# Rotation tables on VectorE, a third convolution buffer and a second buffer of carried states in a two-layer encoder kernel

## The chip, the core and the metric

One core of a Trainium2 chip runs the whole program. The metric is the device time of one execution in microseconds. A core has five engines that run their own instruction streams: TensorE (PE, with its weight loads as PEld), VectorE (DVE), ScalarE (ACT), GpSimd (POOL) and SyncE (SP), whose work here is to issue DMA transfers. An engine runs its instructions in the order in which they were written into its stream; between engines semaphores keep the order.

## The reference

The kernel computes two layers of an encoder over 2048 positions of 1024 features in float32. Only the first layer is touched by the change:

```
h = x + even_layer(rms_norm(x, g0))
even_layer(h):                       # h: [2048, 1024]
    u_a, z_a, v_b, g_b, z_b = split(h @ w_in, 5 x 512)
    y_a = s5(u_a)                    # 32 groups x 16 channels, 64 complex states a group
    y_b = silu(layer_norm(conv31(v_b * sigmoid(g_b)) + conv_b))
    return concat(y_a * silu(z_a), y_b * silu(z_b)) @ w_out
s5(u): s_t = A s_{t-1} + Bbar u_t    # diagonal complex A, per group
       y   = Re(C s) + D u ;  g = gelu(y) ;  return g * sigmoid(g @ w_glu + b_glu)
...
out = rms_norm(h + odd_layer(rms_norm(h, g1)), final_g)   # second layer: sparse attention
```

## The kernel before

The first layer works on the sequence in two halves of 1024 positions (h = 0, 1). `norm(h)` normalises, transposes and splits the rows into a high and a low part (hh, hl), so that a float32 product is made of three matmuls (lines 121 to 123). A projection (`proj`) makes 128 output channels of one half: 8 feature blocks x 2 position blocks x 3 = 48 matmuls of 128x512, into two PSUM tiles ps_p of a pool with four buffers; so a third projection in a row needs that the first one's results have been read. Its weights come in two loads of 256 KB into the staging tile wst (two slots), are cast to wh by ScalarE (line 113) and get their low part wl by a subtraction on GpSimd (line 114), which frees the slot.

The program of half 0 is: `vg(0)` and `vg(1)`, the convolution branch of channel blocks 0 and 1; the tables of the scan, `s5_tables`; four projections `uproj` to uT; the scan `s5_main`; `vg(2)`, `vg(3)`; eight projections `zproj` to zt. In `vg` the gate's projection goes through a sigmoid on ScalarE into sg, the value's projection is multiplied by sg into hc on VectorE, and the convolution is one tensor_scalar and thirty multiply-adds cvo of 128x1024 on VectorE (lines 69 and 72). Where the text says channel 2 it means the channel block of `vg(2)`.

`s5_tables` makes rot, the rotation tables [128, 16, 2, 128] (cosine and sine of the powers), by doubling: in step i the first w columns are rotated by a fixed angle into the next w. It needs four products, one subtraction and one addition per pass, all on GpSimd (`gp_`) before the change; eight passes with w of 1, 2, 4, 8, 16, 32, 32, 32. The scratch tiles ra and rb have one buffer each, under the tags gt and ga; the later tiles q1, q2, and gt and ga of the table quarters, use the same tags. Then come eight quarters: products gt and ga on VectorE, ps_g and ps_h on TensorE, rec on ScalarE, and hs. All is written to HBM (rec_d) and read back by `s5_main` as rg, rt and ry.

`s5_main` takes the input U, which was written to HBM as u_d and read back in eight transfers. For each of eight pairs of groups TensorE makes ps_v, VectorE rotates it by rt (s5t), scans it and rotates it back into sprev (the states at the start of each step, with the carried one in front), and TensorE makes ps_y from sprev and U.

The order of each engine is not the program's: a scheduler orders all engines at build time with a simulated time line, by priority in program order (with a few raised priorities for weight loads, norms, the glu part and the scan of half 1), whenever the tiles that an instruction needs have a free buffer. A changed buffer count or engine so changes the order of all of the first layer. In the second half the same parts follow, with `uproj(1)` and `s5_main(1)` in the middle of the convolution's channels, and with `glu` and `out` at the end. The names in the pool ev, by its tag, are sg, zt, uT, ys and part of xr; the pool is opened in line 446, and sprev in line 534.

Of the kernel before, what the change touches and what calls it, by code (L numbers as in the profile page):

```python
# [11 lines left out]
F32 = mybir.dt.float32  # L12
# [6 lines left out]
ALU = mybir.AluOpType  # L19
# [4 lines left out]
P = 128  # L24
# [6 lines left out]
KC = 128  # L31
# [153 lines left out]
def s5_tables(k, sp, big, ec, S5, rec_d, hs_d, rho, ident, pt):  # L185
# [40 lines left out]
    gp_ = nc.gpsimd  # L226
    for i in range(7):
        m = 1 << i
        w = min(m, 32)
        c0 = cs[:, 1 + i, :, None].to_broadcast([P, 16, w])  # L230
        s0 = sn[:, 1 + i, :, None].to_broadcast([P, 16, w])
        for o in range(0, m, w):
            ra = sp.tile([P, 16, 32], F32, tag="gt", name="ra")[:, :, 0:w]
            rb = sp.tile([P, 16, 32], F32, tag="ga", name="rb")[:, :, 0:w]
            ore = rot[:, :, 0, m + o:m + o + w]
            oim = rot[:, :, 1, m + o:m + o + w]
            ire = rot[:, :, 0, o:o + w]
            iim = rot[:, :, 1, o:o + w]
            k.vtt(ore, ire, c0, ALU.mult, gp_)
            k.vtt(ra, iim, s0, ALU.mult, gp_)  # L240
            k.vtt(oim, ire, s0, ALU.mult, gp_)
            k.vtt(rb, iim, c0, ALU.mult, gp_)
            k.vtt(ore, ore, ra, ALU.subtract, gp_)
            k.vtt(oim, oim, rb, ALU.add, gp_)
    nc.sync.dma_start(
        rec_d[:, :, 768:1024].rearrange("g p c -> p g c"),
        rot.rearrange("p g a c -> p g (a c)"))
# [181 lines left out]
def layer0(k, A, h1_d, ident, vec, dbg):  # L429
# [4 lines left out]
    with ExitStack() as ctx:  # L434
        pool = lambda name, bufs, **kw: ctx.enter_context(tc.tile_pool(name=name, bufs=bufs, **kw))
# [7 lines left out]
        xp = pool("xp", 4)  # L443
        sm = pool("sm", 2)
        pers = pool("pers", 1)
        ev = pool("ev", 2)
        big = pool("big", 3)
        hcp = pool("hcp", 2)
        pt = pool("pt", 2, space=PSUM)
# [14 lines left out]
        pl = {}  # L464
# [63 lines left out]
        def s5_main(h, U, pps):  # L528
            sh = [P, 2, 2, KC]
            for pp in pps:  # L530
                pv = p5.tile(sh, F32, tag="p5v", name="ps_v", bufs=1)
                t1 = pl["s5"].tile([P, 2, 2, 2, KC], F32, tag="s5", name="s5t1")
                w = pl["s5"].tile([P, 2, 2, KC], F32, tag="s5w", name="s5w")
                sp_ = pl["s5"].tile([P, 2, 2, KC + 1], F32, tag="sprev", name="sprev", bufs=1)
                rg = pl["rc"].tile([P, 2, 256], F32, tag="rg", name="rg")
                rt = pl["rc"].tile([P, 2, 256], F32, tag="rt", name="rt")
                ry = pl["rc"].tile([P, 2, 512], F32, tag="ry", name="ry")
                rv = rec_d[2 * pp:2 * pp + 2].rearrange("g p c -> p g c")
                nc.sync.dma_start(rg, rv[:, :, 0:256])
                nc.sync.dma_start(rt, rv[:, :, 768:1024])  # L540
                nc.sync.dma_start(ry, rv[:, :, 256:768])
                for q in range(2):
                    gp = 2 * pp + q
                    for ri in range(2):
                        for eo in range(2):
                            nc.tensor.matmul(
                                pv[64 * eo:64 * eo + 64, q, ri],
                                rg[:, q, ri * 128 + 64 * eo:ri * 128 + 64 * eo + 64],
                                U[:, 2 * gp + eo], start=True, stop=True)
                C = rt[:, :, None, 0:128].to_broadcast(sh)  # L550
                S = rt[:, :, None, 128:256].to_broadcast(sh)
                a, b = t1[:, 0], t1[:, 1]
                win = w
                k.vtt(a, pv, C, ALU.mult)
                k.vtt(b, pv, S, ALU.mult)
                k.vtt(win[:, :, 0], a[:, :, 0], b[:, :, 1], ALU.add)
                k.vtt(win[:, :, 1], a[:, :, 1], b[:, :, 0], ALU.subtract)
                for q in range(2):
                    gp = 2 * pp + q
                    for ri in range(2):  # L560
                        nc.vector.tensor_tensor_scan(
                            out=w[:, q, ri], data0=rho[:, gp:gp + 1].to_broadcast([P, KC]),
                            data1=win[:, q, ri], initial=carry[:, gp, ri:ri + 1],
                            op0=ALU.mult, op1=ALU.add)
                nc.gpsimd.tensor_copy(sp_[:, :, :, 0:1], carry[:, 2 * pp:2 * pp + 2, :, None])
                k.vtt(a, w, C, ALU.mult)
                k.vtt(b, w, S, ALU.mult)
                k.vtt(sp_[:, :, 0, 1:], a[:, :, 0], b[:, :, 1], ALU.subtract)
                k.vtt(sp_[:, :, 1, 1:], a[:, :, 1], b[:, :, 0], ALU.add)
                if h == 0:  # L570
                    nc.gpsimd.tensor_copy(carry[:, 2 * pp:2 * pp + 2, :, None], sp_[:, :, :, KC:])
                uv = U[:, 4 * pp:4 * pp + 4].rearrange("p (q e) c -> p q e c", e=2)
                for eo in range(2):
                    py = p5.tile([P, 2, KC], F32, tag="p5y", name="ps_y", bufs=1)
                    rows = slice(64 * eo, 64 * eo + 64)
                    for q in range(2):
                        nc.tensor.matmul(py[:, q], ry[:, q, 256 + 128 * eo:384 + 128 * eo],
                                         uv[:, q, eo], start=True, stop=False)
                        nc.tensor.matmul(py[:, q], ry[rows, q, 0:128],
                                         sp_[rows, q, 0, 0:KC], start=False, stop=False)  # L580
                        nc.tensor.matmul(py[:, q], ry[rows, q, 128:256],
                                         sp_[rows, q, 1, 0:KC], start=False, stop=True)
                    nc.scalar.activation(uv[:, :, eo], py, AF.Gelu_apprx_tanh)
                if pp % 4 == 3:
                    g0 = (pp // 4) * 16
                    for j in range(NJ):
                        nc.sync.dma_start(
                            g_d[h, g0 * 16:g0 * 16 + 256, j].rearrange("(g c) k -> c g k", c=16),
                            U[16 * j:16 * j + 16, g0:g0 + 16])
# [105 lines left out]
        with tc.tile_pool(name="sp", bufs=1) as sp:  # L695
            s5_tables(k, sp, big, ec, A, rec_d, hs_d, rho, ident, pt)
        pl["s5"] = pool("s5", 2)
        pl["rc"] = pool("rc", 2)
        U = uproj(0, hT)
        s5_main(0, U, range(8))  # L700
        vg(0, hT, cvos[0], 2)
        vg(0, hT, cvos[0], 3)
# [14 lines left out]
        with tc.high_priority(offset=300):  # L717
            s5_main(1, U, range(0, 8))
# [666 lines left out]
def body(tc, A, out, dbg=None, stop=None):  # L1385
    nc = tc.nc
    k = K(tc)
    with ExitStack() as ctx:
        cst = ctx.enter_context(tc.tile_pool(name="cst", bufs=1))
        dpool = ctx.enter_context(tc.tile_pool(name="dscr", bufs=1, space=DRAM))  # L1390
        ident = cst.tile([P, P], F32, name="ident")
        make_identity(nc, ident)
        identr = cst.tile([P, P], F32R, name="identr")
        nc.vector.tensor_copy(identr, ident)
        vec = cst.tile([P, VEC_N], F32, name="vec")
        nc.sync.dma_start(vec, A["vec"])
        dbg = dbg or {}
        scr = lambda n, s, t=F32: dbg[n] if n in dbg else dpool.tile(s, t, name=n + "_d")
        h1_d = scr("h1", [L, D])
        layer0(k, A, h1_d, ident, vec, dbg)  # L1400
        if stop == "l0":
            return
        S = {"q": scr("q", [L, D]), "z": scr("z", [L, D]), "qi": scr("qi", [L, 512]), "att": scr("att", [L, D]),
             "kh": scr("kh", [4, P, L]), "kl": scr("kl", [4, P, L]), "v": scr("v", [L, 256]),
             "mask": scr("mask", [16, P, L], BF16), "sc": scr("sc", [16, P, L]), "hT": scr("hT", [NF, 2, P, HALF])}
        layer1(k, A, h1_d, S, ident, identr, vec)
        layer1_out(k, A, h1_d, S, out, ident)
# [53 lines left out]
```

## Time and profile before

| | us |
|---|---|
| median of three runs | 3005.96 (3002.47 to 3012.47) |
| profiled execution | 3008.15 |
| its span in the trace | 3006.3 |
| TensorE busy in the span | 2754.0 (92%) |
| VectorE busy | 2127.9 (71%) |
| ScalarE busy | 1694.8 (56%) |
| GpSimd busy | 1118.3 (37%) |

The profile's page gives averages over both layers; the change is in the first, whose last projection ends at 703 us, so its stretches are read one by one: windows for how full the engines are, the waits for what an engine stood still for, and the time line for single instructions. A wait of an engine that is not late costs nothing, and a wait is put down to the semaphore that came last.

### The profile page before, as it was taken

Reading aid. Unit: us, or ns where it says so; the run is one execution under the profiler, and the core shown is the slowest. Engines: PE = TensorE matmul, PEld = TensorE weight load, DVE = VectorE, ACT = ScalarE, POOL = GpSimd, SP = SyncE. Lnnn points to the kernel's source line nnn. Section 1 sums busy time; section 2 is a strip of 40 time slices with the busy share of each in tenths; the row PEclk is TensorE's granted clock in tenths of the full one; section 3 lists DMA queues with packets and bytes.
Section 4 is the critical chain, followed back from the end, with each engine's and each line's share of the span. In section 5 each row is a group of like instructions: output and inputs, shape, how many; then the busy total and the mean of one; then the engine's idle time right before and its main releaser. Section 6 shows DMA issues by size and latency. Waiting matters only on the chain.

```text
span 3006.3 us, 47629 instructions
## 1 busy us (share of the span) xinstructions
PE 2754.0 (92%) x17488; PEld 2223.8 (74%) x17488; DVE 2127.9 (71%) x4121; ACT 1694.8 (56%) x3202; POOL 1118.3 (37%) x1453
## 2 busy tenths in 40 slices
PE   7779998799999999899789898999989999999998
PEld 5657786677999898888778885666655666666787
DVE  8889895996354478979997877876777444456444
ACT  4122333334243688778856558888887767655311
POOL 3946132642231587765665323322322101001000
PEclk9889899899999999999899998999999999999999
DMA  3263554356557323223432424110110101001332
GB/s 135 72 131 127 161 158 81 114 168 194 183 186 249 100 71 109 77 84 104 140 109 77 128 92 162 38 57 29 61 38 28 49 18 43 22 5 50 123 126 98
DMA packets 233385, 300.40 MB, mean 100 GB/s; under 512 B 14144, under 2 KB 171072, under 8 KB 233024
## 3 DMA queue, kind: packets, MB, share of 16 engines
q1 hardware_dynamic: 233152, 297.37, 31.5%
q8 instruction: 137, 2.24, 0.3%
q14 instruction: 96, 0.79, 0.1%
HBM read 194.16 MB, written 105.25 MB: 100 GB/s over the span
## 4 chain that ended last, share of the span: by engine, by line
PE 41%; DVE 19%; issue 6%; ACT 5%; POOL 5%; DMA 3%; SPq 0%; DVEq 0%; ACTq 0%; POOLq 0%
PE ps_pv L1133 9%; PE ps_pt L1126 8%; PE ps_s L1095 7%; DVE eq L976 6%; PE ps_tm L121 2%; PE ps_tm L122 2%; PE ps_tm L123 2%; PE ps_o L122 2%; PE ps_o L121 2%; PE ps_o L123 2%; DVE scl L72 2%; POOL sv L69 2%; ACT eq L986 1%; DVE cum L1026 1%; POOL wl L114 1%
## 5 line engine op out<-in xcount | busy, mean ns | idle before, releaser
L114 POOL TENSOR_TENSOR wl<-wst,wh 128x512 fp32r<-128x512 f32 (+1 forms) x220 | 339.0, 1544 | 389.6 <-ACT wh L113 377.8
L121 PE MATMUL ps_tm<-wh,hb 128*128 128x256 f32 (+1 forms) x1536 | 439.4, 290 | 11.7 <-ACT ot L875 7.5
L122 PE MATMUL ps_tm<-wh,hb 128*128 128x256 f32 (+1 forms) x1536 | 444.1, 290 | 0.2 <-DVE hb L72 0.2
L123 PE MATMUL ps_tm<-wl,hb 128*128 128x256 f32 (+1 forms) x1536 | 438.8, 289 | 0.0
L1099 DVE CUSTOM_DVE_ANT_0 lm<-ps_s,amb 128x1024 f32<-128x1024 f32 (+7 forms) x256 | 250.3, 987 | 200.1 <-PE ps_pt L1126 117.2
L72 DVE SCALAR_TENSOR_TENSOR cvo<-hc,vec,cvo 128x1024 f32<-128x1024 f32 x240 | 359.3, 1529 | 0.8
L1131 ACT COPY pT<-ps_pt 128x512 f32<-128x512 f32 (+1 forms) x512 | 273.9, 564 | 152.3 <-PE ps_pt L1126 130.1
L1133 PE MATMUL ps_pv<-pT,v 128*64 128x256 f32 x2176 | 339.3, 398 | 14.4 <-DVE avt L62 7.5
L1126 PEld LDWEIGHTS ps_pt<-ident,lm 128*128 128x128 f32 x2176 | 240.1, 141 | 145.4 <-issue 124.5
L1126 PE MATMUL ps_pt<-ident,lm 128*128 128x128 f32 x2176 | 339.1, 282 | 6.1 <-ACT pT L1131 4.0
L1110 ACT ACTIVATE lm<-lm,mx 128x512 f32<-128x512 f32 (+15 forms) x256 | 309.1, 1211 | 62.9 <-DVE mx L1099 62.4
L69 POOL TENSOR_SCALAR sv<-sv 128x1 f32<-128x1 f32 x448 | 185.5, 415 | 382.6 <-DVE eq L976 296.5
L121 PEld LDWEIGHTS ps_tm<-wh,hb 128*128 128x128 f32 x1536 | 296.2, 194 | 21.2 <-ACT ot L875 9.2
L122 PEld LDWEIGHTS ps_tm<-wh,hb 128*128 128x128 f32 x1536 | 297.7, 194 | 6.0 <-DVE hb L72 0.6
L123 PEld LDWEIGHTS ps_tm<-wl,hb 128*128 128x128 f32 x1536 | 296.4, 194 | 4.8
L113 ACT CAST wh<-wst 128x512 fp32r<-128x512 f32 (+1 forms) x220 | 133.4, 610 | 277.2 <-DMA wst<-in_w_in 122.3
L1095 PE MATMUL ps_s<-kh,qs 128*128 128x512 f32 (+2 forms) x640 | 264.9, 415 | 19.4 <-DVE mx L1099 17.9
L121 PE MATMUL ps_p<-hh,wh 128*128 128x512 f32 x640 | 258.5, 406 | 19.1 <-ACT uT L520 16.0
L123 PE MATMUL ps_p<-hl,wh 128*128 128x512 f32 x640 | 258.9, 407 | 0.0
L122 PE MATMUL ps_p<-hh,wl 128*128 128x512 f32 x640 | 257.5, 403 | 0.0
L1095 PE MATMUL ps_s<-kl,qs 128*128 128x512 f32 (+2 forms) x640 | 233.4, 370 | 0.0
L913 ACT ACTIVATE relu<-ps_i 128x512 f32<-128x512 f32 (+3 forms) x304 | 161.0, 545 | 104.5 <-DVE scl L72 55.3
(327 smaller groups left out, 6353.0 us busy)
## 6 DMA issues: line engine op xcount, KB each, us to landing
wst<-in_w_in SPq DMA_DIRECT2D x168, 256.0 KB, 2.9
zs_d<-zt SPq DMA_DIRECT2D x16, 512.0 KB, 3.5
zt<-zs_d SPq DMA_DIRECT2D x16, 512.0 KB, 4.5
ry<-rec_d SPq DMA_DIRECT2D x16, 512.0 KB, 4.2
xr<-in_x SPq DMA_DIRECT2D x16, 512.0 KB, 4.3
wst<-in_w_out SPq DMA_DIRECT2D x32, 256.0 KB, 3.3
h_d<-xr SPq DMA_DIRECT2D x16, 512.0 KB, 3.5
xt<-h_d SPq DMA_DIRECT2D x16, 512.0 KB, 6.1
```

The source lines that it names most:

```text
L69: eng.tensor_scalar(out=out, in0=a, scalar1=s1, scalar2=s2, op0=op0, op1=op1)
L72: self.nc.vector.scalar_tensor_tensor(out=out, in0=a, scalar=s, in1=b, op0=op0, op1=op1)
L114: nc.gpsimd.tensor_tensor(out=lo, in0=st, in1=hi.bitcast(F32), op=ALU.subtract)
L121: t.matmul(ps, a[0], b[0], start=start, stop=False)
L122: t.matmul(ps, a[1], b[0], start=False, stop=False)
L123: t.matmul(ps, a[0], b[1], start=False, stop=stop)
L1095: nc.tensor.matmul(pss[e][:, cols], qs[e][:, 2 * hp + h], src[:, e, cols], start=part == 0, stop=part == 1)
L1099: self.pace[0] = nc.vector.tensor_tensor_reduce(out=prob[e][h][:, c:c + w], in0=pss[e][:, 0:w], in1=mb[:, c:c + w], scale=-0.125, scalar=( ...
L1110: nc.scalar.activation(lm, lm, AF.Exp, bias=mxs[e, h][:, nh - 1:nh], scale=-1.0, accum_out=t["den"][:, hd:hd + 1])
L1126: nc.tensor.transpose(ps[:, s, h], prob[e][h][:, (b + s) * P:(b + s + 1) * P], ident)
L1131: nc.scalar.copy(pT[:, 0:n], ps[:, 0:n].rearrange("p s h q -> p s (h q)"))
L1133: nc.tensor.matmul(po[64 * s:64 * s + 64, e], self.kvt[(b + s) // 8, kp][2][:, (b + s) % 8, e * 64:e * 64 + 64], pT[:, s], start=b == 0, s ...
```

## The change

The six operations of each doubling pass of rot leave GpSimd for VectorE; the two copies that start the table stay on GpSimd. The pool ev, with the results of the projections that ScalarE evicts for the convolution, the gates and the scan, has three buffers instead of two. The carried states sprev have two instead of one.

```diff
--- before.py
+++ after.py
@@ -236,12 +236,12 @@
             oim = rot[:, :, 1, m + o:m + o + w]
             ire = rot[:, :, 0, o:o + w]
             iim = rot[:, :, 1, o:o + w]
-            k.vtt(ore, ire, c0, ALU.mult, gp_)
-            k.vtt(ra, iim, s0, ALU.mult, gp_)
-            k.vtt(oim, ire, s0, ALU.mult, gp_)
-            k.vtt(rb, iim, c0, ALU.mult, gp_)
-            k.vtt(ore, ore, ra, ALU.subtract, gp_)
-            k.vtt(oim, oim, rb, ALU.add, gp_)
+            k.vtt(ore, ire, c0, ALU.mult)
+            k.vtt(ra, iim, s0, ALU.mult)
+            k.vtt(oim, ire, s0, ALU.mult)
+            k.vtt(rb, iim, c0, ALU.mult)
+            k.vtt(ore, ore, ra, ALU.subtract)
+            k.vtt(oim, oim, rb, ALU.add)
     nc.sync.dma_start(
         rec_d[:, :, 768:1024].rearrange("g p c -> p g c"),
         rot.rearrange("p g a c -> p g (a c)"))
@@ -443,7 +443,7 @@
         xp = pool("xp", 4)
         sm = pool("sm", 2)
         pers = pool("pers", 1)
-        ev = pool("ev", 2)
+        ev = pool("ev", 3)
         big = pool("big", 3)
         hcp = pool("hcp", 2)
         pt = pool("pt", 2, space=PSUM)
@@ -531,7 +531,7 @@
                 pv = p5.tile(sh, F32, tag="p5v", name="ps_v", bufs=1)
                 t1 = pl["s5"].tile([P, 2, 2, 2, KC], F32, tag="s5", name="s5t1")
                 w = pl["s5"].tile([P, 2, 2, KC], F32, tag="s5w", name="s5w")
-                sp_ = pl["s5"].tile([P, 2, 2, KC + 1], F32, tag="sprev", name="sprev", bufs=1)
+                sp_ = pl["s5"].tile([P, 2, 2, KC + 1], F32, tag="sprev", name="sprev", bufs=2)
                 rg = pl["rc"].tile([P, 2, 256], F32, tag="rg", name="rg")
                 rt = pl["rc"].tile([P, 2, 256], F32, tag="rt", name="rt")
                 ry = pl["rc"].tile([P, 2, 512], F32, tag="ry", name="ry")
```

The scheduler then orders the engines anew. VectorE around the start of the scan's tables, before: the products of the convolution's second channel run in one piece, and q (a product of the input matrix with its scale) stands behind them.

```order
L62 TENSOR_TENSOR hc<-ps_p,sg 128x4x128 x2
L72 SCALAR_TENSOR_TENSOR cvo<-hc,vec,cvo 128x1024
L69 TENSOR_SCALAR cvo<-hc,vec 128x1024
L72 SCALAR_TENSOR_TENSOR cvo<-hc,vec,cvo 128x1024 x25
L62 TENSOR_TENSOR q_890<-s5bc,kk 128x256
L72 SCALAR_TENSOR_TENSOR cvo<-hc,vec,cvo 128x1024
L62 TENSOR_TENSOR q_895<-s5bc,kk 128x256
```

After, at the same place, the last pass of rot stands between pairs of these products and ahead of q.

```order
L72 SCALAR_TENSOR_TENSOR cvo<-hc,vec,cvo 128x1024 x2
L62 TENSOR_TENSOR ra<-rot,sn 128x512
L62 TENSOR_TENSOR rb<-rot,cs 128x512
L72 SCALAR_TENSOR_TENSOR cvo<-hc,vec,cvo 128x1024 x2
L62 TENSOR_TENSOR rot<-rot,ra 128x16x32
L62 TENSOR_TENSOR rot<-rot,rb 128x16x32
L72 SCALAR_TENSOR_TENSOR cvo<-hc,vec,cvo 128x1024 x2
L62 TENSOR_TENSOR q_890<-s5bc,kk 128x256
L62 TENSOR_TENSOR q_895<-s5bc,kk 128x256
```

The 48 operations are spread like this over what were unbroken products, and q stands behind all of them.

TensorE around the first table quarter, before: the transposes ps_g stand late in a projection (its seventh feature block, hh_141), which is the gate of channel 2.

```order
L123 MATMUL ps_p<-hl_140,wh 128x512
L121 MATMUL ps_p<-hh_141,wh 128x512
L122 MATMUL ps_p<-hh_141,wl 128x512
L123 MATMUL ps_p<-hl_142,wh 128x512
L330 MATMUL ps_g<-ident,gt 128x128 x4
L352 MATMUL ps_h<-cpr,bd 32x128 x2
L121 MATMUL ps_p<-hh_141,wh 128x512
L122 MATMUL ps_p<-hh_141,wl 128x512
```

After, the gate's projection is finished, and ps_g stands after eleven matmuls of the value's projection of channel 2 (the first feature block, hh_131, and five matmuls of the second).

```order
L123 MATMUL ps_p<-hl_132,wh 128x512
L121 MATMUL ps_p<-hh_133,wh 128x512
L122 MATMUL ps_p<-hh_133,wl 128x512
L123 MATMUL ps_p<-hl_134,wh 128x512
L121 MATMUL ps_p<-hh_133,wh 128x512
L122 MATMUL ps_p<-hh_133,wl 128x512
L330 MATMUL ps_g<-ident,gt 128x128 x4
L352 MATMUL ps_h<-cpr,bd 32x128 x2
L352 MATMUL ps_h<-cpi,bd 32x128 x2
L123 MATMUL ps_p<-hl_134,wh 128x512
```

The first table quarter has moved back by one quarter of a projection and what follows it in the order by as much.

SyncE's queue in the second half, where U is read back, before: eight loads of U in one piece, after one weight load.

```order
L598 DMA gA<-g_d 128x1024 x2
L521 DMA u_d<-uT 128x1024
L106 DMA wst<-in_w_in 128x4x128
L524 DMA U<-u_d 16x32x128 x8
L106 DMA wst<-in_w_in 128x4x128 x2
L539 DMA rg<-rec_d 128x2x256
L106 DMA wst<-in_w_in 128x4x128 x7
```

After, a weight load stands between six and two of them.

```order
L598 DMA gA<-g_d 128x1024 x2
L524 DMA U<-u_d 16x32x128 x6
L106 DMA wst<-in_w_in 128x4x128
L524 DMA U<-u_d 16x32x128 x2
L106 DMA wst<-in_w_in 128x4x128 x2
L539 DMA rg<-rec_d 128x2x256
L106 DMA wst<-in_w_in 128x4x128 x8
```

The loads of U have moved relative to the weight loads, and the first ps_v of this half stands on TensorE behind the whole value projection of channel 1 and five matmuls of the next gate, where before it stood behind fourteen matmuls of that value projection.

## Rows read from the trace of the kernel before

**Rows 1.** Windows: stretch, length, busy us (instructions) per engine, clock, DMA, GB/s.
```profile
320.00:487.00 167.00, 152.58 (x813) 122.54 (x814) 119.67 (x204) 55.64 (x88) 36.61 (x34) 0.92 0.56 144
...
487.00:700.00 213.00, 189.56 (x980) 155.14 (x978) 205.60 (x202) 78.53 (x119) 109.09 (x65) 0.95 0.41 132
```

**Rows 2.** Waits, 100 to 250 us: engine, awaited; total us, times, longest.
```profile
PE ps_p L121 <- ACT uT L520: 16.0, 2, 12.1
...
DVE q L62 <- POOL rot L62: 14.7, 1, 14.7
...
DVE ss L69 <- ACT junk L387: 9.1, 1, 9.1
...
PE ps_g L330 <- DVE gt L62: 8.7, 3, 7.7
```

**Rows 3.** Timeline of ScalarE: start, us, instruction, idle before.
```profile
127.51 0.62 ACT L113 CAST wh<-wst 128x512 fp32r<-128x512 f32 x1 [12.64 <-DMA wst<-in_w_in]
```

**Rows 4.** Timeline of GpSimd, same columns.
```profile
120.34 2.02 POOL L62 TENSOR_TENSOR rb<-rot,cs 128x512 f32<-128x512 f32 x1
...
122.33 2.24 POOL L114 TENSOR_TENSOR wl<-wst,wh 128x512 fp32r<-128x512 f32 x1
...
128.92 1.27 POOL L114 TENSOR_TENSOR wl<-wst,wh 128x512 fp32r<-128x512 f32 x1
```

**Rows 5.** Windows of 10 us, columns of Rows 1.
```profile
100.00:110.00 10.00, 10.00 (x46) 8.29 (x45) 10.00 (x8) 0.07 (x1) 10.00 (x7) 1.00 0.00 0
...
120.00:130.00 10.00, 1.33 (x3) 1.14 (x4) 7.84 (x4) 1.10 (x2) 10.00 (x6) 0.50 0.10 26
```

**Rows 6.** Groups by shape, VectorE, 0 to 500 us.
```profile
L62 DVE TENSOR_TENSOR s5t<-s5w,rt 128x512 f32<-128x512 f32 x16 | 10.3, 683 | 0.1
...
L62 DVE TENSOR_TENSOR gt<-pwr,bbr 128x256 f32<-128x256 f32 x8 | 3.3, 414 | 0.0
...
L62 DVE TENSOR_TENSOR pwt<-pw 128x64 f32<-128x64 f32 x4 | 0.8, 233 | 0.1
```

**Rows 7.** Windows, GpSimd instructions on rot alone.
```profile
0.00:700.00 700.00, 59.21 (x50) 0.93 0.46 131
```

**Rows 8.** Groups by shape, VectorE, 60 to 142 us: busy us, mean ns.
```profile
L72 DVE SCALAR_TENSOR_TENSOR cvo<-hc,vec,cvo 128x1024 f32<-128x1024 f32 x33 | 55.4, 1735 | 0.3
```

**Rows 9.** Groups by shape, VectorE, 145 to 152 us.
```profile
L72 DVE SCALAR_TENSOR_TENSOR cvo<-hc,vec,cvo 128x1024 f32<-128x1024 f32 x5 | 6.4, 1274 | 0.0
```

**Rows 10.** Windows, instructions on wl alone, 69.6 to 142.5 us.
```profile
69.60:142.50 72.90, 31.71 (x78) 15.32 (x77) 14.47 (x9) 0.86 0.16 49
```

**Rows 11.** Timeline of VectorE.
```profile
69.68 11.65 DVE L72 SCALAR_TENSOR_TENSOR cvo<-hc,vec,cvo 128x1024 f32<-128x1024 f32 x7
...
142.50 2.75 DVE L62 TENSOR_TENSOR q<-s5bc,kk 128x256 f32<-128x256 f32 x1 [14.66 <-POOL rot L62]
...
156.90 1.83 DVE L62 TENSOR_TENSOR gt<-gt,ga 128x256 f32<-128x256 f32 x2
...
182.77 1.12 DVE L62 TENSOR_TENSOR hc<-ps_p,sg 128x512 f32<-128x512 f32 x1
...
228.50 2.14 DVE L62 TENSOR_TENSOR hc<-ps_p,sg 128x512 f32<-128x512 f32 x2
...
321.87 1.28 DVE L62 TENSOR_TENSOR s5t<-ps_v,rt 128x512 f32<-128x512 f32 x2
...
487.23 2.12 DVE L62 TENSOR_TENSOR hc<-ps_p,sg 128x512 f32<-128x512 f32 x2 [22.76 <-PE ps_p L123]
```

**Rows 12.** Windows, TensorE instructions of L121 alone.
```profile
0.00:111.00 111.00, 44.93 (x112) 21.68 (x112) 0.98 0.30 101
...
0.00:267.00 267.00, 105.32 (x257) 50.87 (x258) 0.91 0.40 111
```

**Rows 13.** Waits, 400 to 550 us.
```profile
PE ps_v L546 <- DMA wst<-in_w_in: 11.4, 1, 11.4
```

**Rows 14.** Timeline of SyncE's queue.
```profile
455.12 8.40 SPq L524 DMA_DIRECT2D U<-u_d  x8
```

## The prediction

> **What bounds the kernel now.** The windows come first. The first layer's projections fill the first 700 us; from 487 to 700 us VectorE is busy 205.60 of 213 us, while from 320 to 487 us it works only 119.67 of 167, and TensorE 152.58 [rows 1]. So no single engine sets the first layer's end: a saving counts if it moves TensorE's projections and, behind them, the VectorE stretch that starts at 487 us.
>
> The waits of TensorE between 100 and 250 us show where it stands still: 16.0 us in two waits for uT, the longest 12.1, and 8.7 us for gt, the longest 7.7; VectorE itself loses 14.7 us in one wait, for rot on GpSimd [rows 2]. The wait for uT is named after ScalarE, but ScalarE's row shows that it stood 12.64 us before the cast wh that precedes the copy, waiting for a weight load [rows 3]. The load needed a staging slot, the slot is released by the subtraction wl on GpSimd, and wl stands in GpSimd's queue behind rotation operations of 2.02 us; one wl took 2.24 us there and the next, with VectorE idle, 1.27 us [rows 4]. So one queue, GpSimd's, makes TensorE wait for weights and VectorE for the scratch tiles ra and rb, whose slots q1 and q2 reuse. After the wait TensorE pays once more: its granted clock is 0.50 between 120 and 130 us, 1.2 of 2.4 GHz, and the three matmuls there took 1.33 us, 0.44 each, while 46 fit into the 10 us from 100 to 110, 0.22 each [rows 5].
>
> **What the change moves, and its price.** The 48 operations of the rotation tables go from GpSimd to VectorE's program order, where the order shows them between the products cvo of the second channel. The sizes are 18 of 128x512, and six each of 256, 128, 64, 32 and 16 elements. VectorE's own rows: 0.683 us for a 512 product of two SBUF operands, 0.414 for 256, and 0.233 for 64 [rows 6]. The sum: 18 x 0.683 = 12.3; 6 x 0.414 = 2.5; 24 smaller ones at the price of 64 elements, 5.6; together 20.4. I take 19, since twelve of the 24 have only 32 or 16 elements. The upper end, since no row shows these operations on VectorE, is GpSimd's own mean, 59.21/50 = 1.18 us [rows 7], thus 57 us for the 48.
>
> Given back on VectorE: the wait of 14.7. Then contention: 33 products averaged 1.735 us while GpSimd ran tables, against 1.274 in a stretch beside less of it [rows 8, 9]; 33 x 0.46 = 15.2 us. Not all goes, because the nine wl of that stretch, 14.47 us [rows 10], stay on GpSimd. A wl beside a product was about 1 us longer than alone [rows 4], and I charge the products the same: nine are 9 us that stay, 6.2 go.
>
> The Trainium skill (SBUF — State Buffer, "Who interferes with whom") says that a VectorE operation with two SBUF inputs and a GpSimd operation that reads SBUF exclude each other for a whole instruction; the doubling above agrees. It speaks against part of this change, for wl reads SBUF, and the new rotation products have two SBUF inputs as well; by it an estimate is that nine wl each still cost up to one product, 9 x 1.27 = 11.4 us, and the gain would be 2.4 us smaller than mine.
>
> Now along the time axis. The first products start at 69.68 and q1 at 142.50, the first complete gt at 156.90, 14.4 us later [rows 11]. After the change the order puts 26 products (33.0 us at 1.27), two gate products hc (2.3), the tables (19) and the 9 us of contention ahead of q1: 69.7 + 63.3 = 133. The first gt comes at 147.4.
>
> TensorE has done seven projections at 111 us (112 matmuls of L121, 16 each) [rows 12]. Without the late wl the eighth (u of channel 3) needs 48 x 0.227 = 10.9 us, the gate of channel 2 as much, and the order then has eleven matmuls of its value before the first ps_g: 135.5. It waits 12 us for gt there, so the wait for gt grows from 7.7 while that for uT goes. Behind it: 37 matmuls and the two table blocks at a lowered clock, about 13 us, then gate and value of channel 3 at 12.5 each: 185.5.
>
> The next bound is a PSUM slot: the first z projection takes the slots that hc of channel 2 frees. That hc ended at 182.77 + 1.12 = 183.9 [rows 11]. After: + 19 - 14.7 - 6.2, and + 5.5 because the order puts one more table quarter and the statistics of the second norm before it: 187.5. TensorE waits 2. The fourth z projection needs hc of channel 3, which ended at 230.6 [rows 11]. After: + 19 - 14.7 - 6.2 - 9.1 (a wait of ss for ScalarE's squares, of which the later start of this step leaves nothing [rows 2]) + 10.6 (14 more table operations at 0.41 = 5.8, four normalisations of xb at 0.9, an estimate of three quarters of a product, and small ones): 230.2. Three z projections from 187.5 end at 222.5, so TensorE waits 7 more, and the fourth ends at 241.5, where it ended at 266.6 before (16 projections, 256 of the row's 257 matmuls [rows 12]). TensorE leads by 25 us.
>
> Not all is kept. Between hc of channel 3 and the first scan operation, at 321.87 [rows 11], VectorE was nearly full. The order leaves 41 of 48 products there, and takes out the four normalisations and about a dozen table operations: 91 us become 75, and s5t starts at 306, 16 us earlier, while TensorE is 25 earlier. I take 20, between the two. In the second half, the first ps_v waits 11.4 us for the U loads (the trace names a weight load; the queue's row shows U's eight loads at 455.12, 8.40 us of issue) [rows 13, 14]. The new order puts all of the value projection of channel 1 and five matmuls of the next gate before it, which cover some 4 us: 24. From 487 us VectorE has the same work in both orders and only starts earlier, and from 700 us the order of TensorE, the fuller engine, is unchanged, so the 24 stay to the end.
>
> The two buffer counts I cost at nothing by themselves: the scans run where VectorE has idle time [rows 1], and no wait in the rows names a slot of ev or the carried states. They do make the scheduler place scan and projections differently; bounds for that are -5 and +5 us.
>
> Sum: 3008.15 - 24 = 2984 against the profiled execution, which lies 2.2 above the median of the runs, 3005.96. Forecast 2982.
>
> **Rivals.**
> 1. The lead is kept whole and the U wait vanishes: 25 + 11.4 = 36 us, 2970. For it: VectorE idles 47 of the 167 us from 320 on [rows 1], room to make up its 9 us. Against it: U's loads still follow a transfer through HBM whose time doesn't depend on any compute engine.
> 2. The lead is lost behind 266 us, no change: the waits only change names. From 487 us VectorE is full, and if the lead in TensorE is eaten by s5t, by U and by the weights' staging slots, what is left is the 16 us of s5t less a second wait for U as long as the 11.4 of now, since two of its loads stand behind a weight load in the new queue order and TensorE asks sooner: 4.6 us, 3001. For it: VectorE's own balance in this stretch is only 19 against 14.7 + 6.2. That the buffers don't do what they should counts here: no row asks for them.
> 3. Slower: a rotation operation costs on VectorE what it cost on GpSimd, 1.18 us, because its operands are broadcast and strided. Then 57 us instead of 19 stand before hc of channel 3, which ends at 268; the fourth z projection ends at 279, 12 later than before, and the program takes 3018. It decides from an hc at 255 on, that is from 44 us for the tables, 0.92 each. For it: q's first product, also with a broadcast operand, took 2.75 us at 142.50 [rows 11]; against it: gt has a broadcast operand as well and takes 0.414 [rows 6].
>
> **How the numbers follow.** The forecast's case, 2972 to 2992, has 0.47; rival 1, below, 0.19; rival 2 with what lies around no change 0.22; rival 3 0.12. A measurement of this kernel can tell about 0.3%, 9 us, from no change, so faster means below 2997: 0.47 + 0.19 and a sliver of rival 2, 0.68; same 0.20; slower 0.12. The range takes in rivals 1 and 2 and the ends of the contention and of the buffers, but not rival 3: 2958 to 3011. The likeliest case's own range is 2972 to 2992.
>
> **What would show it.** Right: rotation operations of 512 on VectorE at 0.6 to 0.75 us; wl on GpSimd at no more than 2.3 us and never behind anything but bd and its like; no wait for uT above 4 us before 130; ps_g waiting 10 to 14 us for gt once; q1 at about 133; the fourth z projection ending near 241; s5t near 306; the hc that stood at 487.23 near 463. Wrong: a table operation at 1 us or more, an hc of channel 3 after 240, or a U wait above 15 us in the second half. If the lead at 487 is there and the time isn't, it was given back in the glu stage, and ps_g's waits there would show it.

## The result and the profile after

The changed kernel takes 2990.44 us (2987.48 to 2993.87) where the one before takes 3003.91 in the same comparison: a ratio of 0.9949, 95% interval 0.9934 to 0.9964, some 15 us faster by the ratio and 13.5 by the medians. The profiled executions are 2989.37 and 3008.15 us, 18.8 apart; the forecast was 24 apart. The sign, the mechanism in the first 130 us and the range held; the size was too large.

The page's first lines after, busy time by engine:

```profile
span 2987.6 us, 47596 instructions
...
PE 2745.3 (92%) x17488; PEld 2217.5 (74%) x17488; DVE 2124.0 (71%) x4169; ACT 1683.9 (56%) x3194; POOL 1072.3 (36%) x1405
```

GpSimd has 46 us less work than the 1118.3 of before, VectorE about as much. The windows that answer to [rows 1], and those that count TensorE's instructions of line 121, as [rows 12]:

```profile
320.00:487.00 167.00, 153.99 (x819) 124.08 (x818) 135.18 (x216) 54.25 (x85) 43.63 (x37) 0.96 0.52 127
487.00:700.00 213.00, 186.33 (x1015) 153.82 (x1013) 195.39 (x218) 70.78 (x116) 119.41 (x66) 0.93 0.46 149
```

```profile
0.00:122.00 122.00, 51.35 (x129) 25.02 (x130) 0.99 0.35 118
0.00:247.00 247.00, 104.34 (x257) 50.40 (x257) 0.94 0.44 122
0.00:267.00 267.00, 114.59 (x283) 55.32 (x284) 0.94 0.44 124
```

Eight projections (128 matmuls) are done at 122 us, sixteen (256) at 247, where the row of before has 257 only at 267: TensorE leads by 20 us. At 267 it is 26 matmuls ahead.

The waits from 100 to 250 us, to be read beside [rows 2]:

```profile
ACT junk L387 <- DMA xb<-in_x: 11.0, 1, 11.0
DVE ss L69 <- ACT junk L387: 10.1, 1, 10.1
...
PE ps_g L330 <- DVE gt L62: 8.2, 2, 7.3
PE ps_h L352 <- POOL bd L312: 8.1, 1, 8.1
```

The wait for uT (16.0) and that of q for rot (14.7) are gone from the view. The wait for gt is one of 7.3. What has stayed is ss, the sums of squares of the rows xb (the last 512 positions of the second half, being normalised), behind ScalarE's squares: 10.1 us. A new wait stands on TensorE's path: ps_h, a product of the table quarters, waits 8.1 us for its operand bd, which GpSimd copies. It has the same origin, as ScalarE's, GpSimd's and TensorE's rows show:

```profile
166.76 1.06 ACT L387 ACTIVATE junk<-xb 128x1024 bf16<-128x1024 f32 x1 [11.04 <-DMA xb<-in_x]
...
170.34 0.60 ACT L113 CAST wh<-wst 128x512 fp32r<-128x512 f32 x1
```

```profile
171.07 1.26 POOL L114 TENSOR_TENSOR wl<-wst,wh 128x512 fp32r<-128x512 f32 x1 [1.89 <-ACT wh L113]
172.28 0.86 POOL L312 COPY bd<-bbr 64x32 f32<-64x32 f32 x2
```

```profile
172.87 0.64 PE L352 MATMUL ps_h<-cpi,bd 128*32 128x128 f32 x4 [8.11 <-POOL bd L312]
```

ScalarE stands 11.04 us for the transfer of xb, the cast wh comes behind the squares, wl waits for wh, and bd stands behind wl in GpSimd's queue.

VectorE's time line, to be read beside [rows 11]:

```profile
131.81 0.76 DVE L62 TENSOR_TENSOR q<-s5bc,kk 128x256 f32<-128x256 f32 x2
...
141.66 0.76 DVE L62 TENSOR_TENSOR gt<-gt,ga 128x256 f32<-128x256 f32 x2
...
172.02 0.34 DVE L69 TENSOR_SCALAR ss<-ss 128x4 f32<-128x4 f32 x1 [10.09 <-ACT junk L387]
...
194.08 2.09 DVE L62 TENSOR_TENSOR hc<-ps_p,sg 128x512 f32<-128x512 f32 x2
...
232.92 2.12 DVE L62 TENSOR_TENSOR hc<-ps_p,sg 128x512 f32<-128x512 f32 x2
...
307.56 1.28 DVE L62 TENSOR_TENSOR s5t<-ps_v,rt 128x512 f32<-128x512 f32 x2
...
447.63 1.13 DVE L62 TENSOR_TENSOR hc<-ps_p,sg 128x512 f32<-128x512 f32 x1 [0.65 <-PE ps_p L123]
```

q starts at 131.81 (142.50 before), the pair that completes the first gt at 141.66 (156.90), s5t at 307.56 (321.87) and the hc of 487.23 at 447.63, earlier than the 463 of the forecast; the next two pairs of hc come 24.0 and 25.9 us earlier (490.09 for 514.11, 550.29 for 576.21). But hc of channel 2 ends later than before, at 196.2 instead of 183.9, because ss now stands ahead of it and waits. TensorE waits only 2.2 us for that hc.

The rotation operations on VectorE: all of them, and two shapes.

```profile
0.00:700.00 700.00, 21.82 (x48) 0.94 0.48 137
```

```profile
L62 DVE TENSOR_TENSOR rot<-rot,sn 128x512 f32<-128x512 f32 x3 | 2.0, 683 | 0.0
...
L62 DVE TENSOR_TENSOR rot<-rot,ra 128x128 f32<-128x128 f32 x1 | 1.4, 1382 | 0.0
```

48 operations are 21.82 us, 0.683 for a 512 as the neighbouring row had it; four small ones took 1.28 to 1.38 us beside a wl. Last, where the lead went. In the second half of the layer TensorE waits for a weight's low part:

```profile
PE ps_p L122 <- POOL wl L114: 20.0, 4, 16.3
PE ps_v L546 <- DMA U<-u_d: 13.0, 1, 13.0
```

```profile
510.63 17.20 POOL L114 TENSOR_TENSOR wl<-wst,wh 128x512 fp32r<-128x512 f32 x1 [9.37 <-ACT wh L113]
```

```profile
507.26 8.45 DVE L72 SCALAR_TENSOR_TENSOR cvo<-hc,vec,cvo 128x1024 f32<-128x1024 f32 x7
515.63 2.00 DVE L62 TENSOR_TENSOR zt<-zt,cvo 128x1024 f32<-128x1024 f32 x1
517.53 1.28 DVE L72 SCALAR_TENSOR_TENSOR cvo<-hc,vec,cvo 128x1024 f32<-128x1024 f32 x1
518.73 2.00 DVE L62 TENSOR_TENSOR zt<-zt,cvo 128x1024 f32<-128x1024 f32 x1
520.64 6.07 DVE L72 SCALAR_TENSOR_TENSOR cvo<-hc,vec,cvo 128x1024 f32<-128x1024 f32 x5
...
537.75 2.50 DVE L62 TENSOR_TENSOR zt<-zt,cvo 128x1024 f32<-128x1024 f32 x1 [11.04 <-DMA zt<-zs_d]
```

One wl on GpSimd, 1.27 us when it is alone [rows 4], took 17.20 us, from 510.63 to 527.83. In that time VectorE ran products of two SBUF operands without a break, at 1.2 us each (8.45 for seven, 6.07 for five), as if nobody stood beside it. The last of them ended at 526.7, VectorE then stood idle for 11.04 us, and the wl was through 1.1 us after that moment. Before, no wl there was kept out like this: the longest operation on GpSimd between 487 and 700 us was a product zt of 128x256, 8.85 us at 552.50, beside eleven products of VectorE in one piece.

The output projection's matmuls by the two kernels, before and then after (duration min, median, max; first and last start):

```profile
L121 PE MATMUL ps_tm<-wh,hh x512: 277/283/415, 706.2 to 953.5; 128*128 128x256 f32 x171
```

```profile
L121 PE MATMUL ps_tm<-wh,hh x512: 277/283/579, 681.2 to 935.9; 128*128 128x256 f32 x171
```

They start 25.0 us earlier and end 17.6 earlier, and from there on both kernels have one order and about keep that distance: the spans differ by 18.7. TensorE's windows of this stage are 248.0 us with 240.04 busy before and 255.5 with 243.91 after: 3.9 us is work that the kernel before had done ahead of it, 3.6 are waits.

### The profile page after: what moved, and what is told of

Read it like the earlier page. It is cut to its first block, busy times and chain, and to the rows that moved or that the text cites. A ratio compares the mean times of both kernels' runs of the same rounds, so it can differ in the third digit from the quotient of the medians.

```text
span 2987.6 us, 47596 instructions
## 1 busy us (share of the span) xinstructions
PE 2745.3 (92%) x17488; PEld 2217.5 (74%) x17488; DVE 2124.0 (71%) x4169; ACT 1683.9 (56%) x3194; POOL 1072.3 (36%) x1405
## 4 chain that ended last, share of the span: by engine, by line
PE 48%; DVE 25%; issue 8%; POOL 7%; DMA 6%; ACT 5%; SPq 2%; DVEq 0%; ACTq 0%; POOLq 0%
PE ps_pv L1133 9%; PE ps_pt L1126 8%; PE ps_s L1095 7%; DVE eq L976 6%; DVE cvo L72 4%; PE ps_p L122 2%; PE ps_p L121 2%; PE ps_p L123 2%; PE ps_o L122 2%; PE ps_o L121 2%; PE ps_o L123 2%; POOL wl L114 2%; PE ps_tm L121 2%; POOL sv L69 2%; PE ps_tm L122 2%
## 5 line engine op out<-in xcount | busy, mean ns | idle before, releaser
L114 POOL TENSOR_TENSOR wl<-wst,wh 128x512 fp32r<-128x512 f32 (+1 forms) x220 | 362.6, 1652 | 396.8 <-ACT wh L113 366.5
L121 PE MATMUL ps_tm<-wh,hb 128*128 128x256 f32 (+1 forms) x1536 | 439.8, 291 | 11.6 <-ACT ot L875 8.2
L72 DVE SCALAR_TENSOR_TENSOR cvo<-hc,vec,cvo 128x1024 f32<-128x1024 f32 x240 | 344.6, 1464 | 0.9
L121 PEld LDWEIGHTS ps_tm<-wh,hb 128*128 128x128 f32 x1536 | 296.3, 194 | 21.4 <-ACT ot L875 9.5
L1095 PE MATMUL ps_s<-kh,qs 128*128 128x512 f32 (+2 forms) x640 | 265.0, 415 | 18.4 <-DVE mx L1099 16.8
L121 PE MATMUL ps_p<-hh,wh 128*128 128x512 f32 x640 | 256.2, 403 | 6.7 <-ACT hh L406 2.7
```

The source lines that it names most:

```text
L72: self.nc.vector.scalar_tensor_tensor(out=out, in0=a, scalar=s, in1=b, op0=op0, op1=op1)
L114: nc.gpsimd.tensor_tensor(out=lo, in0=st, in1=hi.bitcast(F32), op=ALU.subtract)
L121: t.matmul(ps, a[0], b[0], start=start, stop=False)
L1095: nc.tensor.matmul(pss[e][:, cols], qs[e][:, 2 * hp + h], src[:, e, cols], start=part == 0, stop=part == 1)
```

## Experiments

Each was measured beside the kernel before on one chip. The table has the ratio to that kernel and its 95% interval. The experiments ran on four chips, where the kernel before had medians from 3002.13 to 3005.65 us, so experiments are set against the change and each other by their ratios; 0.001 is 3 us. The last column is the start of the last output matmul of the first layer in the profiled execution. It is a single value, but free of the second layer, which no edit touches and which took 2042 to 2056 us in these executions.

| kernel | median us | ratio | interval | layer 1 ends, us |
|---|---|---|---|---|
| before | 3003.91 | 1 | | 953.5 |
| the change | 2990.44 | 0.9949 | 0.9934 to 0.9964 | 935.9 |
| 1 rotation on VectorE alone | 2987.73 | 0.9938 | 0.9915 to 0.9960 | 934.8 |
| 2 both buffer counts alone | 2999.12 | 0.9977 | 0.9961 to 0.9992 | 946.9 |
| 3 ev alone | 3008.09 | 1.0005 | 0.9989 to 1.0020 | 955.6 |
| 4 wl on VectorE, rotation on GpSimd | 2998.93 | 0.9979 | 0.9965 to 0.9992 | 945.6 |
| 5 sprev alone | 2991.58 | 0.9970 | 0.9960 to 0.9981 | 944.9 |
| 6 change without rotation | 2990.90 | 0.9963 | 0.9951 to 0.9975 | 943.7 |
| 7 change, products of rotation twice | 2990.62 | 0.9962 | 0.9951 to 0.9974 | 944.0 |
| 8 change, wl of one z projection on VectorE | 2977.09 | 0.9918 | 0.9906 to 0.9930 | 924.2 |
| 9 as 6, twelve wl on VectorE | 2980.26 | 0.9924 | 0.9909 to 0.9939 | 925.5 |
| 10 change, xb loads early | 2976.43 | 0.9916 | 0.9901 to 0.9931 | 927.2 |
| 11 as 8, U loads early | 2980.63 | 0.9931 | 0.9911 to 0.9950 | 928.9 |
| 12 as 8 and 10 together | 2973.92 | 0.9885 | 0.9855 to 0.9915 | 924.8 |

Every edit makes the scheduler order the first layer anew, so a wait can come or go that the edit was not meant for. In experiments 1, 3, 4, 6, 7, 9 and 10, as in the change, TensorE waits 15.0 to 16.3 us for one long wl between 490 and 535 us; in the kernel before and in experiment 5 such a wait is under 1 us, and in 2 it is 3.7.

**The parts of the change.** Experiment 1 takes the first hunk of the change's diff alone, 2 the other two, 3 only

```diff
-        ev = pool("ev", 2)
+        ev = pool("ev", 3)
```

and 5 only

```diff
-                sp_ = ... name="sprev", bufs=1)
+                sp_ = ... name="sprev", bufs=2)
```

> Only the rotation tables move to VectorE; ev keeps two buffers and sprev one. Theory A (GpSimd's queue made the weights late, and the buffers are worth nothing by themselves): 13 to 17 us faster than before, the eighth projection (u of channel 3) ends at 121 to 123 us instead of 142, and the whole change's gain is here within 4 us. Theory B (the buffers carry the gain by letting the scheduler place the scan earlier): less than 8 us faster.

> Only the buffer counts change (ev three, sprev two); the rotation tables stay on GpSimd. Theory A: within 5 us of before, the eighth projection still ends at about 142 us and the wait for uT of some 12 us is still there. Theory B: at least 8 us faster.

> Only ev has three buffers. Theory A: within 5 us of before. Theory B, if the convolution's results are what the buffers serve: 5 to 12 us faster, with the first z projections earlier.

> Only sprev has two buffers. The two buffer counts together gave a ratio of 0.9977, ev alone 1.0005. Theory A, that the second sprev buffer carries what the buffers give: 4 to 10 us faster than before. Rival D, that the buffers only shuffle the scheduler's order and the gain of both is luck of that order: within 4 us of before.

The rotation alone gives the whole gain, some 18 us, and its count of line 121 says so where the wait was:

```profile
0.00:122.00 122.00, 52.32 (x130) 25.06 (x130) 0.99 0.35 118
0.00:267.00 267.00, 114.71 (x286) 55.26 (x286) 0.96 0.43 124
```

Eight projections are done at 122 us. With the buffers alone the waits of [rows 2] stand as before, and the gain is about 7 us. ev gives nothing in the time, but its run has a long wl that the kernel before does not have:

```profile
512.96 19.89 POOL L114 TENSOR_TENSOR wl<-wst,wh 128x512 fp32r<-128x512 f32 x1 [4.58 <-ACT wh L113]
```

TensorE waits 15.0 us for it, so what ev is worth without it is not shown. sprev alone gives 9, by the interval 6 to 12, against the forecast's nothing. Up to 500 us its projections end within 6 us of those before. Its output stage starts 3.1 us earlier than before (703.1 for 706.2) and ends 8.6 earlier, so most of its gain comes late; which wait it takes away there was not settled, and a luckier order (the reason that Rival D gives) is not excluded. On top of the rotation the buffers add nothing that shows: the intervals of 1 and of the change overlap, and the change's own is the less favourable. Theory A holds for the rotation; that a buffer is worth nothing by itself was wrong for sprev.

**Was it the weights?** In experiment 4 the rotation stays on GpSimd and the wl of six projections leave it (twelve, where the expectation says ten):

```diff
-    def load_w(self, src, f0, nf, c0, ncol, wp, stage=2, into=None):
+    def load_w(self, src, f0, nf, c0, ncol, wp, stage=2, into=None, eng=None):
...
-                nc.gpsimd.tensor_tensor(out=lo, in0=st, in1=hi.bitcast(F32), op=ALU.subtract)
+                (eng or nc.gpsimd).tensor_tensor(out=lo, in0=st, in1=hi.bitcast(F32), op=ALU.subtract)
...
-            for tb, ps in enumerate(proj(hT, c * P)):
+            for tb, ps in enumerate(proj(hT, c * P, None if h else nc.vector)):
```

and the same in `vg` for channel 2 of half 0.

> The kernel before with one edit: the ten weight low parts wl of the four u projections and of gate and value of channel 2 in half 0 are made on VectorE, the rotation tables stay on GpSimd. Theory A, that a late wl behind the rotation operations is what stops TensorE at 116 to 128 us: the eighth projection ends before 126 us and the wait for uT falls below 4 us, while q on VectorE still waits for rot, ending near 128 to 135 us; 5 to 15 us faster in all. Rival C, that the gain of the change came from VectorE (the wait of q and the contention) and not from the weights: the wait for uT goes too, but the time is within 4 us of before, since VectorE, with 7 us more work, reaches the gate products no earlier than now.

```profile
PE ps_g L330 <- DVE gt L62: 16.8, 1, 16.8
...
DVE q L62 <- POOL rot L62: 13.3, 1, 13.3
```

The wait for uT is gone, so it was the late wl; but the eighth projection still ends at 142 us. The scheduler put the first ps_g into it, and TensorE waits there 16.8 us for gt, which waits for q, which waits 13.3 for rot. 6 us are gained. It could have been more: the fourth z projection ends at 253.2 us (266.4 before), and then TensorE waits for a long wl that the kernel before does not have:

```profile
PE ps_p L122 <- POOL wl L114: 15.9, 1, 15.9
```

So both halves of GpSimd's queue mattered, the weights and the scratch tiles, and the change removes both: neither A nor C alone.

**Is VectorE's added work on the path?** Experiment 6 leaves the rotation out, 7 does its products twice:

```diff
+    nc.gpsimd.memset(rot, 1.0)
...
-            k.vtt(ore, ire, c0, ALU.mult)
...
-            k.vtt(oim, oim, rb, ALU.add)
```

```diff
             k.vtt(ore, ire, c0, ALU.mult)
             k.vtt(ra, iim, s0, ALU.mult)
             k.vtt(oim, ire, s0, ALU.mult)
             k.vtt(rb, iim, c0, ALU.mult)
+            (the four lines again)
```

> The changed kernel without the 48 rotation operations: rot is filled with ones, its transfer and all that reads it stay. VectorE loses 21.8 us of work ahead of the gate products. Theory A, that VectorE's work ahead of q and of the gate products of channels 2 and 3 sets where TensorE stands: the first ps_g comes at about 120 to 125 us and waits under 2 us, the program is 8 to 20 us faster than the changed kernel (2970 to 2982). Rival E, that after the change the next waits (the xb transfer behind ScalarE's squares, the U loads) set the pace, whatever VectorE does: within 5 us of the changed kernel, 2985 to 2995.

> The changed kernel with the four products of each of the eight rotation passes done twice: 32 more operations on VectorE, some 14 us, all before q. Theory A (VectorE's work there is on the path): 8 to 14 us slower than the changed kernel, 2998 to 3005. Rival E (other waits set the pace): within 5 us of it.

Taking away 21.82 us of VectorE's work and adding 16.1 (37.88 in all) come to the same: by their ratios each is about 4 us slower than the change, with intervals that overlap its own, and the first layer ends 8 us later in both. For experiment 6 that is against Theory A. For 7 it lies between the 8 to 14 us of Theory A and the 5 of Rival E, and does not decide between them. For 6 there is a reason beside rival E's. Without the rotation GpSimd's time line has

```profile
90.94 16.77 POOL L114 TENSOR_TENSOR wl<-wst,wh 128x512 fp32r<-128x512 f32 x1 [3.80 <-ACT wh L113]
...
133.04 13.25 POOL L114 TENSOR_TENSOR wl<-wst,wh 128x512 fp32r<-128x512 f32 x1
```

two wl of 16.77 and 13.25 us, and u of channel 2 ends at 124 us instead of 111. Experiment 9 tests that: the same kernel, with the wl of the four u projections and of channel 2 on VectorE by the edit of experiment 4.

> The kernel without the 48 rotation operations (rot filled with ones), with the low parts wl of the four u projections and of gate and value of channel 2 in half 0 on VectorE instead of GpSimd. Without rotations two wl took 16.77 and 13.25 us on GpSimd, and the gain was nothing against the changed kernel. Theory H, that these two locked-out wl ate the gain: u of channel 2 ends at 111 us instead of 124, the eighth projection near 122, channel 3's value before 185, and the fourth z projection 8 us or more earlier than the 264 us without this edit; 3 to 12 us faster than without it (2979 to 2988). Rival E (other waits set the pace whatever happens here): the projections end earlier by 100 to 140 us, but the time is within 3 us of 2991.

The time falls by some 12 us against 6 (10.6 by the medians; the intervals of 6 and 9 are apart), inside Theory H's forecast, and the fourth z projection ends at 253.5 us. But u of channel 2 ends at 116 and not 111 us and the eighth projection at 129 and not 122: the next operation in GpSimd's queue, a bd, was then the one that took 15.69 us. So without the rotation and with those wl on VectorE the kernel is 8 us faster than the change by the ratios (10 by the medians, intervals overlapping); without the rotation alone nothing of this is left, because GpSimd is kept out. How much of it the moved wl would give with the rotation in place was not run.

**The one long wl in the changed kernel.** Experiment 8 makes the two low parts of one projection on VectorE, with experiment 4's parameter:

```diff
-            for tb, ps in enumerate(proj(hT, (512 if br == 0 else 2048) + c * P)):
+            for tb, ps in enumerate(proj(hT, (512 if br == 0 else 2048) + c * P, nc.vector if (h, br, c) in ((1, 0, 0),) ...
```

> The changed kernel with the two weight low parts wl of the first z projection of half 1 made on VectorE; one of them took 17.20 us on GpSimd at 510.63 us while VectorE ran its products without a break, and TensorE waited 16.3 us for it. Theory F, that TensorE is the path there: the wait goes, and the program is 5 to 14 us faster than the changed kernel. Rival G, that from 487 us on VectorE is the path, so that a wait of TensorE there costs nothing: within 4 us of the changed kernel, although the wait goes.

```profile
PE ps_p L122 <- POOL wl L114: 3.8, 2, 1.9
```

The wait of 16.3 us is gone, the projection ends at 527 instead of 544 us, and the program is 9 us faster than the change by the ratios (13 by the medians, which stand on two chips); the intervals are apart, and the first layer ends 11.7 us earlier. The two subtractions took 0.68 and 1.23 us on VectorE. Theory F holds, and with it the forecast's view that VectorE bounds this stage falls (rival G).

**The squares behind xb.** Experiment 10 raises the priority of half 1's loads of x (of the four of xt, which stay at 31 us, and of the four of xb), so that xb's stand ahead of seven U loads:

```diff
-                    with tc.high_priority(offset=0 if h or j else 2500):
+                    with tc.high_priority(offset=2500 if h or not j else 0):
```

> The changed kernel with the four xb loads of half 1 ahead of seven of the eight U loads in SyncE's queue (a raised priority). Theory I, that ScalarE's 11 us at the squares, waiting for xb, and VectorE's 10.1 us behind it are what made hc of channel 2 end at 196 instead of the 187.5 that was forecast: VectorE's wait for the squares falls below 3 us, that hc ends before 190, the fourth z projection before 243 (247 in the changed kernel), and the program is 3 to 7 us faster than the changed kernel. Rival J, that bd behind the weights' low parts on GpSimd (ps_h waited 8.1 us for it) holds TensorE there anyway: the wait for the squares goes, but the fourth z projection stays within 2 us of 247 and the time within 3 us.

```profile
156.89 0.15 DVE L69 TENSOR_SCALAR ss<-ss 128x4 f32<-128x4 f32 x1
...
186.65 2.12 DVE L62 TENSOR_TENSOR hc<-ps_p,sg 128x512 f32<-128x512 f32 x2
```

```profile
0.00:247.00 247.00, 107.51 (x266) 51.60 (x267) 0.96 0.44 123
```

ss no longer waits, hc of channel 2 ends at 188.8 us (the forecast for the change was 187.5), 266 matmuls are done at 247 us and the fourth z projection ends at 240 (forecast 241.5). The program is 10 us faster than the changed kernel by the ratios (14 by the medians; the intervals are apart, and the first layer ends 8.7 us earlier), more than Theory I asked for. Rival J falls: the wait of ps_h for bd is gone with the wait for the squares, as it must be if bd was late because of them.

**Two more.** Experiment 11 adds to 8 a raised priority for half 1's U loads, and 12 puts 8 and 10 together.

```diff
+                with tc.high_priority(offset=3000 if h else 0):
                     nc.sync.dma_start(U[16 * j:16 * j + 16],
```

> The kernel with the first z projection's low parts on VectorE (2977.09 us, ratio 0.9918), and the U loads of half 1 ahead of the weight load in SyncE's queue. Theory F (TensorE is the path from 448 to 550 us): the first ps_v of half 1 waits for U less than 10 us instead of 13, and the time falls by what is saved, 2 to 6 us. Rival K: U's loads wait for u_d's transfer and not for their place in the queue; the wait stays at 11 to 14 us and the time within 3 us of 2977.

```profile
PE ps_v L547 <- DMA U<-u_d: 14.2, 1, 14.2
```

The eight loads stand in one piece, and the wait is 14.2 us. So it is not the place in the queue; so far Rival K is right. Its reason, u_d's transfer, does not fit the rows: u_d's last store was issued at 426.83 us and took 2.7 us to land. U's loads, issued from 440.58 us on, wait 1.8 us for the stores g_d that read the U before, and then take a median of 11.3 us each to land.

> The changed kernel with both edits that helped: xb's loads ahead of seven of U's (2976.43 us alone) and the first z projection's low parts of half 1 on VectorE (2977.09 us alone). If the two waits that they remove are one behind the other on TensorE's path, the gains add: some 14 and 13 us off the changed kernel's 2990.44, 2962 to 2968. If the layer's end is by then set by VectorE from 487 us on or by the out stage, the second edit gives little on top: 2972 to 2977.

```profile
PE ps_p L122 <- POOL wl L114: 18.9, 4, 13.2
```

This has the lowest ratio of all, 0.9885, but the interval (0.9855 to 0.9915) reaches the two parts, and the first layer ends no earlier than in experiment 8 (924.8 us for 924.2). The profile shows a reason why the gains don't add: a wl of the next projection now takes 18.37 us, and TensorE waits 13.2 us for that one.

## Why the prediction came out right in sign and too large in size

- **GpSimd's queue.** Right. The wait for uT and that of q go, the eighth projection ends at 122 us as computed, q starts at 131.8 (133). Experiment 1 puts the whole gain there.
- **The price of the rotation.** 21.8 us for 19, by the four small ones that ran beside a wl. They are over the 1 us that was named as a sign of being wrong, but too few to matter. Rival 3, GpSimd's price on VectorE, falls: 0.45 us each, not 1.18.
- **The first gt.** 147.4 was computed, and 141.7 measured: the order had put q's two products side by side, and fewer operations up to gt. TensorE waits 7.3 for 12.
- **The step that failed: "a wait of ss for ScalarE's squares, of which the later start of this step leaves nothing", 9.1 us.** It is 10.1 us, because xb's loads stand behind U's on SyncE's queue and came some 20 us earlier (the first was issued at 150.83 us for 170.65), by no more than VectorE did. The working counted the statistics ahead of hc of channel 2, at their price but without their wait, and took the wait out further on. So hc ended at 196.2, not 187.5. That by itself cost TensorE no more than was forecast: it waited 2.2 us for that hc, where the working has 2. What made TensorE late is a second branch of the same wait, which the working does not have at all: ScalarE's cast wh stood behind the squares, wl and bd behind the cast, and ps_h waited 8.1 us for bd. TensorE came to the first z projection at 193.0 us, not 185.5, and its lead at the fourth was 20 us and not 25. Experiment 10 brings xb's loads forward; both waits go, and it lands on the computed times, 188.8 and 240.
- **U's wait, 4 us to be covered.** 13.0 us, against 11.4 before: nothing was covered. TensorE was ready for it 15.2 us earlier than before, and the wait ended 13.6 us earlier.
- **The contention, taken as 1 us a wl.** For most of them it is: 2.1 to 2.3 us beside a product, 1.3 alone. But three took 7.24, 10.17 and 17.20 us, against the 2.3 that was named as the sign of being right. The last stood on TensorE's path and cost 9 to 13 us (experiment 8). It is the largest term that was missing. With it gone the gain over the kernel before is 25 us; that this is the forecast's 24 is chance, for the wait of the step above is still in it.
- **From 487 us on VectorE sets the pace.** Wrong: 195.39 busy of 213 after, and a wait of TensorE there costs most of its length (experiment 8: 16.3 us of wait, 11.7 us at the end of the first layer). The lead was also not kept through the output stage, 25.0 at its start and 17.6 at its end. The 25.0 looks like the forecast's 24, but is luck in part: the long wl lies before it, and the change has done less of TensorE's work by then (2941 matmuls, 2977 before).
- **The buffers at nothing.** No gain from ev was seen. sprev alone is worth 9 us, outside the bounds of 5, and on top of the rotation the two add nothing that shows.

The chances: the sign had 0.68, and the median of 2990.44 lies at the upper edge of the likeliest case, 2972 to 2992. Two unforeseen waits, of 8.1 and 16.3 us on TensorE, went against it and a wait for gt of 7.3 instead of 12 went for it; the rest of the balance is not accounted for, so that the range held is in part luck. Rival 2, that the lead is eaten by new waits, came closer to what happened than rival 1, but through GpSimd and xb, and not through s5t.

## What to carry to other kernels

An engine that is 37% busy can still hold two others up, when short operations that free a buffer stand behind a run of other work in its queue; look for the operation that frees the slot, not at the engine that the wait names. When work leaves such a queue for a full engine, list every wait of the second one again, in the new order, with what stands behind it on every engine: the wait that depended on a transfer stayed here (10.1 us for 9.1), and it reached TensorE through ScalarE's and GpSimd's queues. And what remains on the first engine may now run beside an unbroken stretch of two-operand work, and can be kept out for many operations.

## What was not expected of the hardware

A GpSimd subtraction of 128x512 with two SBUF operands takes 1.27 us alone and about 2.2 beside a single VectorE product of 1.27. But it was kept out for as long as 17.20 us in the changed kernel, 10.88 in the kernel before (at 217.67), 16.77 without the rotation and 19.89 with ev alone, while VectorE's operations ran at their undisturbed pace. The two others of the changed kernel are

```profile
155.85 7.24 POOL L114 TENSOR_TENSOR wl<-wst,wh 128x512 fp32r<-128x512 f32 x1 [7.04 <-ACT wh L113]
...
205.39 10.17 POOL L114 TENSOR_TENSOR wl<-wst,wh 128x512 fp32r<-128x512 f32 x1 [4.24 <-ACT wh L113]
```

In the changed kernel each of the three long ones ended some 1.2 us after VectorE paused: at 163.09, when VectorE had stopped at 161.9 for the squares; at 215.56, when it had stopped at 214.4 for ps_h; at 527.83, when it had stopped at 526.7 for a load of zt. A pause is not always needed, as GpSimd's and VectorE's rows of the kernel before show:

```profile
217.67 10.88 POOL L114 TENSOR_TENSOR wl<-wst,wh 128x512 fp32r<-128x512 f32 x1
```

```profile
227.31 1.26 DVE L72 SCALAR_TENSOR_TENSOR rs<-rsqt,rs 128x4 f32<-128x4 f32 x1
```

There VectorE had not stopped; an operation of 128x4, 0.15 us elsewhere, took 1.26, and the wl ended at 228.55, as if it had got its turn ahead of that one. The Trainium skill (SBUF — State Buffer, "Who interferes with whom") says that one of the two blocks for a whole instruction; the doubled times agree, but in the long cases GpSimd lost its turn some ten times in a row. That an unbroken run of VectorE makes it so is read from these rows, and was not tried by itself; why most wl get through after one product, at 2.2 us, and a few do not stays open.
